# Gate and up of an FFN by seven quarter products, with the order of three engines written out

## The chip, the cores and the metric

One core of a Trainium2 chip runs the whole program in one launch. The metric is the device time of the program in microseconds, from runs on the chip; the profile is one more execution, recorded by the hardware profiler. The core has five engines with queues of their own: TensorE (PE, with its weight loads as PEld), VectorE (DVE), ScalarE (ACT), GpSimd (POOL) and SyncE (SP); here SP and POOL mainly issue transfers.

## The reference

A decoder trunk of two layers, 512 tokens of 1024 features, float32. Layer 0 has a state-space mixer, layer 1 an attention; each is followed by the same gated FFN with 2816 inner features. Only the FFN is touched:

```python
def conv_ffn(h, w_up, conv_w, conv_b, w_down):
    gu = h @ w_up
    g = gu[..., :D_FF]
    u = gu[..., D_FF:]
    g = lax.conv_general_dilated(      # causal, width 3, each feature for itself
        g, conv_w, ..., feature_group_count=D_FF) + conv_b
    return (jax.nn.silu(g) * u) @ w_down
...
x = x + conv_ffn(rms_norm(x, norm_ffn[layer]), ...)
```

After layer 0 a shared key and value are projected from x; after layer 1 a last RMSNorm gives the output.

## The kernel before

Everything is stored feature by token: `x` is 8 tiles of 128 features by 512 tokens. Every matrix product is done to float32 precision by three float32r matmuls for each 128x128 block: an operand is split into a high part (a ScalarE CAST, `split_hi`, L161, or a copy) and a low part (a VectorE subtraction, `split_lo`, L166), and `gemm` (L171) adds high x high, high x low and low x high in a PSUM bank. All these matmuls have line L112 in the profile, all two-input VectorE operations L118 (`tt`) or L115 (`stt`), the CASTs of weights L163.

The 2816 inner features are 22 tiles `f` of 128, handled in three chunks of 8, 7 and 7 (`FF_CHUNKS`). For each tile of a chunk the gate weights `wg` (128 x 1024, 512 KB) are loaded on SP's queue into one of three raw buffers, split, and multiplied with the eight split tiles of x (`bg`, tile fg: 24 matmuls of 512 columns); then the same for up (`wu`, `bu`, tile fu). VectorE multiplies the gate by the RMS factor `rb` of each token (g), ScalarE and VectorE run the filter (acc: one ScalarE operation, two VectorE ones), ScalarE the SiLU (s), VectorE multiplies by rb and s (u), and the product is split again (ah, al) as input of the down product. After a chunk, eight down products (`wd`, tile fd) take the chunk's 8 or 7 tiles as inputs, and each is added to one of the tiles of x. In the last chunk each finished x tile is handed on at once: to the squares for the next norm, and to its own split.

In all this the order of each engine's instructions, and which buffer is reused when, comes from a scheduler that the program runs through when it is built. Two places have an order written out by hand (`tc.manual_schedule`): the sweep of attention, and the end of the kernel, `Final.last` (L1371), where the last two down products are cut into halves of the sequence so that norm and output of the first half run beside the products of the second. Split weights live in rings of three buffers for the high and three for the low parts (pool `wp`): a fourth split waits until TensorE is done with the first.

Of the kernel before, what the change touches and what calls it, by code (L numbers as in the profile page):

```python
# [17 lines left out]
P = 128  # L18
# [1 line left out]
KT = 8  # L20
NH = 16
FT = 22
FF_CHUNKS = ((0, 8), (8, 15), (15, 22))
EPS = 1e-6
AW = 22
TP = {"ta": 10}
# [21 lines left out]
def trunk(ctx: ExitStack, tc: tile.TileContext, A, out):  # L48
# [49 lines left out]
    def wide(name, n, tag):  # L98
        pool, bufs = cur["w"]
        return pool.tile([P, n * S], F32, tag=tag, name=name, bufs=bufs[tag])  # L100

    def N(name, tag, bufs):
# [14 lines left out]
    def tt(o, a, b, op, eng=None):  # L117
        (eng or V).tensor_tensor(out=o, in0=a, in1=b, op=op)  # L118
# [694 lines left out]


    def ffn(layer, prev, st_next):
        with Work(f"ff{layer}", {"g": "la", "s": "lb", "u": "lc"}, a=24, acc=2, y=1, half=6):
            banks_by_tag(b=7, st=1)
            rb, _ = prev.st.finish()
            ffn_body(layer, prev.xs, rb, st_next)

    def ffn_body(layer, xs, rb, st_next):
        cw = const.tile([P, FT, 4], F32, name="cw")
        nc.scalar.dma_start(out=cw, in_=A["conv"][layer])
        for ci, (f0, f1) in enumerate(FF_CHUNKS):
            acts = []
            for f in range(f0, f1):
                wg = load_split(A["w_up"][layer, f, 0], 8, name="wg")
                bg = B("fg")
                gemm(bg, wg, xs)
                wu = load_split(A["w_up"][layer, f, 1], 8, name="wu")  # L830
                bu = B("fu")
                gemm(bu, wu, xs)
                g = T("g", tag="g")
                tt(g, bg, rb, MUL)
                acc = T("acc", tag="acc")
                SC.activation(out=acc, in_=g, func=AF.Identity, scale=cw[:, f, 2:3], bias=cw[:, f, 3:4])  # L836
                stt(acc[:, 1:], g[:, :S - 1], cw[:, f, 1:2], acc[:, 1:], MUL, ADD)
                stt(acc[:, 2:], g[:, :S - 2], cw[:, f, 0:1], acc[:, 2:], MUL, ADD)
                s = T("s", tag="s")
                SC.activation(out=s, in_=acc, func=AF.Silu)  # L840
                u = T("u", tag="u")
                tt(u, bu, rb, MUL)
                tt(u, u, s, MUL)
                ah, al = T("ah", F32R, "a"), T("al", F32R, "a")
                SC.copy(out=ah, in_=u)
                tt(al, u, ah, SUB)
                acts.append((ah, al))
            for n in range(KT):
                w = load_split(A["w_dn"][layer, n][:, f0 * P:f1 * P], f1 - f0, name="wd")
                if f1 == FT and n == KT - 2 and hasattr(st_next, "last"):  # L850
                    st_next.last((w, load_split(A["w_dn"][layer, KT - 1][:, f0 * P:f1 * P], f1 - f0, name="wd")), acts)
                    return
                bd = B("fd")
                gemm(bd, w, acts)
                tt(x[:, n], x[:, n], bd, ADD)
                if ci == len(FF_CHUNKS) - 1:
                    st_next(n)


    def attention(prev, st_next):  # L860
# [495 lines left out]
    class Final:  # L1356
# [7 lines left out]
        def __call__(self, n):  # L1364
            self.st.add(n)
            if n == 0:
                tc.keep_in_program_order(SC.preload_act_table_set("abs_reciprocal_sqrt_and_small"))
                self.y = wide("yo", KT, "y").rearrange("p (k t) -> p k t", k=KT)
            SC.activation(out=self.y[:, n], in_=x[:, n], func=AF.Copy, scale=gcol(NFIN, n))

        def last(self, ws, acts):  # L1371
            n0, H, K = KT - 2, S // 2, len(acts)
            halves = [slice(0, H), slice(H, S)]
            sq6, sq7, v, r, q, rr = (T(t, tag="half") for t in ("sq6", "sq7", "v7", "r7", "q7", "rr7"))
# [40 lines left out]
            with tc.manual_schedule(engines={E.PE, E.DVE, E.Activation}):  # L1415
# [2 lines left out]
                gathered(n0, 0)  # L1418
                product(n0 + 1, 0)
                added(n0 + 1, 0)  # L1420
                mm(total[:, halves[0]], ones, acc[:, halves[0]], True, False)
                product(n0, 1, 0, 5)
                mm(total[:, halves[0]], ones, sq[n0 + 1][:, halves[0]], False, True)
                root(0)
                product(n0, 1, 5, K)
                newton(0)
                added(n0, 1)
                gathered(n0, 1)
                scaled(0, 0, 4)
                send(0, 0, 4, nc.sync)  # L1430
                product(n0 + 1, 1, 0, 4)
                mm(total[:, halves[1]], ones, acc[:, halves[1]], False, False)
                product(n0 + 1, 1, 4, K)
                added(n0 + 1, 1)
                scaled(0, 4, 6)
                send(0, 4, 6, nc.sync)
                mm(total[:, halves[1]], ones, sq[n0 + 1][:, halves[1]], False, True)
# [91 lines left out]
```

## Time and profile before

| | |
|---|---|
| median of 3 runs | 1229.63 us (1229.43 to 1229.68) |
| profiled execution | 1230.19 us |
| its span, first to last instruction | 1228.4 us |
| TensorE busy | 1204.6 us, 98% of the span |
| VectorE busy | 804.0 us, 65% |
| ScalarE busy | 546.0 us, 44% |
| GpSimd busy | 24.0 us, 2% |
| moved by DMA | 118.47 MB, 96 GB/s over the span |
| clock granted to TensorE | 0.998 |

In the profile FFN layer 0 lies at 222 to 584 us, attention at 584 to 853 us, FFN layer 1 from 853 us to the end. A row of the groups gives line, engine, operation, output<-inputs, shape, count, then busy time and mean duration of one, then the idle time before it and what ended that. A row of the chain or of the instructions in order of time gives start and duration in us. A matmul's duration contains its way through the array, so that of neighbours overlaps; the distance between their starts tells what each costs.

### The profile page before, as it was taken

The page shows a single profiled execution, that of the slowest core. Times are in us where ns is not written, and L with a number is a line of the kernel's source. Part 1 is how long each engine was busy: PE and PEld are TensorE (multiplying, and loading weights), DVE is VectorE, ACT ScalarE, POOL GpSimd, SP SyncE. Part 2 cuts the span into 40 slices and gives each one's busy share as a digit, 9 for nine tenths or more (in the row PEclk, how much of TensorE's full clock was granted, in tenths as well). Part 3 has the DMA queues.
Part 4 walks back from the last instruction along what each step waited for, and adds up shares of the span by engine and source line. Part 5 has one row for each costly group of instructions (what it writes and reads, how often), then busy time and mean ns, then how long its engine had stood idle before and what let it go on. Part 6 is the DMA issues. An engine that isn't in the chain of part 4 may idle for free.

```text
span 1228.4 us, 16234 instructions
## 1 busy us (share of the span) xinstructions
PE 1204.6 (98%) x6434; PEld 984.1 (80%) x6434; DVE 804.0 (65%) x1254; ACT 546.0 (44%) x881; POOL 24.0 (2%) x65
## 2 busy tenths in 40 slices
PE   7999999999999999999999999999999999999996
PEld 3467788788888888888889898988888888888885
DVE  7999665655445635657878989878655346536554
ACT  5245453433223323334577878765433233313341
POOL 1011010000000000000000000000000000000000
PEclk9999999999999999999999999999999999999999
DMA  5565342223333233233211211123233332332322
GB/s 195 157 174 146 111 136 89 89 98 103 89 100 103 81 108 103 87 96 104 68 52 54 82 52 51 39 86 103 87 103 93 96 103 85 91 116 86 97 76 69
DMA packets 55037, 118.47 MB, mean 96 GB/s; under 512 B 12881, under 2 KB 28497, under 8 KB 54961
## 3 DMA queue, kind: packets, MB, share of 16 engines
q1 hardware_dynamic: 50304, 105.02, 28.2%
q0 software_dynamic: 3248, 11.54, 3.1%
q8 instruction: 50, 0.82, 0.3%
q10 hardware_dynamic: 1408, 0.88, 0.2%
q14 instruction: 27, 0.21, 0.1%
HBM read 109.03 MB, written 8.39 MB: 96 GB/s over the span
## 4 chain that ended last, share of the span: by engine, by line
PE 88%; DVE 8%; ACT 1%; issue 1%; DMA 1%; DVEq 0%; SPq 0%; ACTq 0%
PE fu L112 19%; PE fd L112 19%; PE fg L112 19%; PE gl L112 6%; PE kqb L112 6%; PE ob L112 5%; PE z L112 5%; PE v L112 4%; PE u L112 2%; DVE k L118 2%; DVE p L118 1%; PE y L112 1%; DMA x<-in_xT 1%; DVE cm L118 1%; ACT xg L282 1%
## 5 line engine op out<-in xcount | busy, mean ns | idle before, releaser
L112 PE MATMUL fd<-ah,wdh 128*128 128x512 f32 (+1 forms) x366 | 140.0, 382 | 0.0
L112 PE MATMUL fd<-al,wdh 128*128 128x512 f32 (+1 forms) x366 | 139.4, 381 | 0.0
L112 PE MATMUL fd<-ah,wdl 128*128 128x512 f32 (+1 forms) x366 | 139.4, 381 | 0.0
L118 DVE TENSOR_TENSOR x<-x,fd 128x512 f32<-128x512 f32 (+1 forms) x50 | 33.3, 665 | 116.6 <-PE fd L112 116.6
L163 ACT CAST wuh<-wur 128x1024 fp32r<-128x1024 f32 x44 | 46.3, 1053 | 134.0 <-PE fg L112 117.8
L163 ACT CAST wdh<-wdr 128x896 fp32r<-128x896 f32 (+1 forms) x48 | 47.2, 983 | 123.8 <-PE fd L112 91.5
L118 DVE TENSOR_TENSOR g<-fg,rb 128x512 f32<-128x512 f32 x44 | 30.4, 691 | 96.3 <-PE fg L112 93.6
L112 PE MATMUL fu<-xh,wuh 128*128 128x512 f32 x220 | 86.0, 391 | 0.0
L112 PE MATMUL fg<-xh,wgl 128*128 128x512 f32 x220 | 85.7, 389 | 0.0
L112 PE MATMUL fu<-xl,wuh 128*128 128x512 f32 x220 | 85.6, 389 | 0.0
L112 PE MATMUL fg<-xh,wgh 128*128 128x512 f32 x220 | 85.6, 389 | 0.0
L112 PE MATMUL fu<-xh,wul 128*128 128x512 f32 x220 | 85.6, 389 | 0.0
L112 PE MATMUL fg<-xl,wgh 128*128 128x512 f32 x220 | 85.6, 389 | 0.0
L118 DVE TENSOR_TENSOR u<-fu,rb 128x512 f32<-128x512 f32 x44 | 30.4, 691 | 80.5 <-PE fu L112 80.5
L112 PE MATMUL fu<-xhl,wuh 128*128 128x512 f32 x264 | 81.9, 391 | 0.0
L112 PE MATMUL fg<-xhl,wgh 128*128 128x512 f32 x264 | 81.6, 389 | 0.0
L112 PEld LDWEIGHTS fd<-ah,wdh 128*128 128x128 f32 x366 | 68.8, 188 | 13.3
L112 PEld LDWEIGHTS fd<-ah,wdl 128*128 128x128 f32 x366 | 68.8, 188 | 13.3
L112 PEld LDWEIGHTS fd<-al,wdh 128*128 128x128 f32 x366 | 68.8, 188 | 13.2
L163 ACT CAST wgh<-wgr 128x1024 fp32r<-128x1024 f32 x44 | 46.3, 1053 | 70.1 <-PE fd L112 32.6
L112 PE MATMUL u<-xg,wi 128*128 128x512 f32 x128 | 64.0, 635 | 7.3 <-ACT xg L282 7.3
L115 DVE SCALAR_TENSOR_TENSOR acc<-g,cw,acc 128x511 f32<-128x511 f32 x88 | 65.7, 747 | 2.5 <-ACT acc L836 0.9
(250 smaller groups left out, 2798.0 us busy)
## 6 DMA issues: line engine op xcount, KB each, us to landing
wgr<-in_w_up SPq DMA_DIRECT2D x44, 512.0 KB, 3.5
wur<-in_w_up SPq DMA_DIRECT2D x44, 512.0 KB, 3.5
wdr<-in_w_dn SPq DMA_DIRECT2D x32, 448.0 KB, 3.3
wdr<-in_w_dn SPq DMA_DIRECT2D x16, 512.0 KB, 3.5
wvr<-in_w_glu POOLq DMA_DIRECT2D x12, 512.0 KB, 3.8
ks<-kx SPq DMA_DIRECT2D x32, 128.0 KB, 2.5
m<-ks SPq DMA_DIRECT2D x8, 512.0 KB, 4.3
awr<-in_w_k SPq DMA_DIRECT2D x8, 512.0 KB, 3.4
```

The costliest lines, as they stand in the source:

```text
L112: PE.matmul(o, lhsT=lhsT, rhs=rhs, start=start, stop=stop, skip_group_check=True)
L115: (eng or V).scalar_tensor_tensor(out=o, in0=a, scalar=s, in1=b, op0=op0, op1=op1)
L118: (eng or V).tensor_tensor(out=o, in0=a, in1=b, op=op)
L163: SC.copy(out=hi, in_=raw)
L282: SC.activation(out=xg.rearrange("p (j c) -> p j c", j=8), in_=by_step(x[:, k]), func=AF.Copy, scale=gcol(NMIX0, k))
```

## The change

Five of the 22 tiles of a layer stay as they were (`Plain`). For the other 17 (`Seven`) gate and up are computed together. With the inner sum cut into two halves of four x tiles, the weights of a tile are four quarters of 128 x 512: A and B (gate), C and D (up). With the tokens cut into two halves of 256, the 2 x 2 block product of quarters and halves of x needs eight products of quarters in the plain way; the change uses a scheme with seven, on sums:

- Weight sums. `Diag` loads A and D side by side by one transfer on SP (`wdg`); their difference is a VectorE subtraction (`differ`), split into dd. `Sum` makes C+A and C+D (`wsa`), and A+B and B+D (`wsb`), by two transfers on POOL's queue: one loads C (or B) twice, and a second, accumulating one (`accum_op=ADD`) adds A and D to it in SBUF. Sums have three buffers of their own (tag sr).
- Sums of x. `form_sums(k)`, for k = 0 to 3, normalizes tiles k and k+4 of x (gain and rb) and forms seven sums and differences of their quarters, 256 columns each; `form_hi` and `form_lo` split them into `fh` and `fl`. It runs beside the plain tiles.
- Products. `first` to `fifth` issue seven products of 4 x 3 matmuls with 256 columns into halves of two banks (f0, f1); some accumulate on the result of an earlier one. VectorE and ScalarE join them to g and u (`sum1`, the ends of `second` and `fourth`, `join`). rb is already in the sums.
- Chunks are now 4, 5, 4, 5 and 4 tiles (`FF_ENDS`), so there are 40 down products with 4 or 5 inputs per layer in place of 24 with 7 or 8. The down products of a chunk are no longer done in one go: four of the first chunk's stand behind the first four tiles, the others stand among the changed tiles of the next chunk (`da` between second and third, `db` at the end), two of the fourth chunk's behind them, and the last chunk's eight end the layer as before.
- The order of TensorE, VectorE and ScalarE is written out from the second plain tile to the end of the changed ones. The loads stay three ahead of the splits (`ahead`).
- In `Final.last` the output and scratch tiles use the buffers of fh and fl, and the order of a few steps is another: the first half's scaling and sending stand behind the products of the second.

```diff
-FF_CHUNKS = ((0, 8), (8, 15), (15, 22))
+FF_ENDS = (4, 9, 13, 18, 22)
...
+        def quarters(f, rows, half, step):
+            o = A["w_up"][layer, f, rows, :, half * Q:half * Q + Q]
+            return bass.AP(o.tensor, o.offset, [[KT * P, P], [step, 2], [1, Q]])
+        diag = P * KT * P + Q
...
+        class Diag(Weight):
...
+            def load(self):
+                self.raw = self.tile()
+                nc.sync.dma_start(out=self.raw.rearrange("p (h c) -> p h c", h=2), in_=quarters(self.f, 0, 0, diag))
+            def differ(self):
+                self.d, dd = T("d", tag="s"), pair("dd")
+                tt(self.d, self.raw[:, 0:Q], self.raw[:, Q:], SUB)
+                self.dw = dd[:, 0:S], dd[:, S:]
...
+        class Sum(Weight):
...
+            def load(self):
+                self.raw = self.tile()
+                t2 = self.raw.rearrange("p (h c) -> p h c", h=2)
+                GP.dma_start(out=t2, in_=quarters(*self.at, 0))
+                GP.dma_start(out=t2, in_=quarters(self.at[0], 0, 0, diag), accum_op=ADD)
+
+        def form_sums(k):
+            q, c = (pair(n, F32).rearrange("p (s c) -> p s c", s=4) for n in ("fq", "fc"))
+            gain = NFFN0 if layer == 0 else NFFN1
+            for i, kk in ((1, k), (0, k + 4)):
+                stt(q[:, i::2], x[:, kk].rearrange("p (s c) -> p s c", s=2), gcol(gain, kk),
+                    rb.rearrange("p (s c) -> p s c", s=2), MUL, MUL)
+            tt(c[:, 0:2], bc(q[:, 1], 1, [P, 2, H]), q[:, 2:4], ADD)
+            tt(c[:, 2], q[:, 3], q[:, 2], SUB)
+            tt(c[:, 3], q[:, 0], q[:, 2], ADD)
+            tt(q[:, 0], q[:, 0], q[:, 1], SUB)
+            form_sums.parts = k, ((c, slice(3, 7)), (q[:, 0:3], slice(0, 3)))
...
+        class Seven(Act):
+            def __init__(self, f, ci):
+                super().__init__(f, ci)
+                self.s1, self.r = Sum(f, 1, 0, "wsa"), Diag(f)
+            def later(self):
+                self.s2 = Sum(self.f, 0, 1, "wsb")
+            def prod(self, o, wt, s, first=False, last=True):
+                gemm(o, wt, [(fh[:, k, s], fl[:, k, s]) for k in range(4)], k1=4,
+                     first=None if first else False, last=None if last else False)
+            def first(self):
+                b0, b1 = B("f0"), B("f1")
+                self.up1, self.gate2, self.m17, self.n6 = b0[:, 0:H], b0[:, H:], b1[:, 0:H], b1[:, H:]
+                self.prod(self.up1, self.s1.part(1), 1, True, False)
+                self.prod(self.gate2, self.r.part(0), 5, False, False)
+                m, tw, self.u = (T(n, tag="u") for n in ("m3", "tw", "u"))
+                self.t, self.wv = tw[:, 0:H], tw[:, H:]
+                SC.copy(out=m[:, 0:H], in_=self.gate2)
+                self.m = m
+            def sum1(self):
+                tt(self.t, self.up1, self.m[:, 0:H], ADD)
+            def second(self):
+                self.prod(self.m17, self.r.dw, 3, True, False)
+                self.prod(self.n6, self.s1.part(0), 4)
+                tt(self.wv, self.m17, self.t, ADD)
+                tt(self.u[:, H:], self.n6, self.wv, SUB)
+            def third(self):
+                self.prod(self.up1, self.r.part(1), 0)
+            def fourth(self):
+                self.prod(self.gate2, self.s2.part(0), 2)
+                self.g = T("g", tag="g")
+                SC.copy(out=self.g[:, H:], in_=self.gate2)
+                tt(self.t, self.t, self.up1, SUB)
+                tt(self.t, self.t, self.gate2, SUB)
+            def fifth(self):
+                self.prod(self.m17, self.s2.part(1), 6)
+            def join(self):
+                tt(self.g[:, 0:H], self.m17, self.t, ADD)
...
+            for t, nxt in zip(sevens, sevens[1:] + [None]):
+                if prev:
+                    prev.mul()
+                if t.da:
+                    t.da.w.hi()
...
+                else:
+                    t.s2.lo()
+                    t.first()
+                    if prev:
+                        prev.split()
+                    t.sum1()
+                if prev:
+                    prev.low()
...
+                t.second()
...
+                if t.da:
+                    t.da.step()
+                    t.da.add()
+                t.third()
+                if t.db:
+                    t.db.w.both()
+                if nxt:
+                    nxt.s1.hi()
+                t.fourth()
+                if nxt:
+                    nxt.s1.lo()
+                t.fifth()
+                if nxt:
+                    nxt.r.hi()
+                    nxt.r.differ()
+                t.join()
+                t.filter0()
+                if t.db:
+                    t.db.step()
+                if nxt:
+                    nxt.r.lo()
+                    nxt.r.differ_hi()
+                    if not nxt.da:
+                        nxt.s2.hi()
+                t.filter()
+                if nxt:
+                    nxt.r.differ_lo()
+                prev = t
```

Three places of the new order, each before and after. L118 and L115 of the kernel before are L122 and L119 of the changed one, and L918 and L919 are the two transfers of `Sum.load`.

First, VectorE in the middle of a chunk of layer 0. Before, one gate-and-up tile after another:

```order
L118 TENSOR_TENSOR g<-fg,rb 128x512
L118 TENSOR_TENSOR wul<-wur,wuh 128x1024
L115 SCALAR_TENSOR_TENSOR acc<-g,cw,acc 128x511
L115 SCALAR_TENSOR_TENSOR acc<-g,cw,acc 128x510
L118 TENSOR_TENSOR u<-fu,rb 128x512
L118 TENSOR_TENSOR u<-u,s 128x512
L118 TENSOR_TENSOR wgl<-wgr,wgh 128x1024
L118 TENSOR_TENSOR al<-u,ah 128x512
```

Now, from the end of one changed tile with one down product into the next (f_2956 and f_2957 are its two banks, wsa the next tile's first sum, wdg its diagonal quarters, d and dd their difference):

```order
L122 TENSOR_TENSOR tw<-tw,f_2956 128x256 x2
L122 TENSOR_TENSOR wsal<-wsar,wsah 128x1024
L122 TENSOR_TENSOR d<-wdgr 128x512
L122 TENSOR_TENSOR g<-f_2957,tw 128x256
L122 TENSOR_TENSOR wdgl<-wdgr,wdgh 128x1024
L119 SCALAR_TENSOR_TENSOR acc<-g,cw,acc 128x511
L119 SCALAR_TENSOR_TENSOR acc<-g,cw,acc 128x510
L122 TENSOR_TENSOR dd<-d,dd 128x512
L122 TENSOR_TENSOR u<-f_2956,s 128x256
L122 TENSOR_TENSOR u<-u,s 128x256
L122 TENSOR_TENSOR wsbl<-wsbr,wsbh 128x1024
```

The splits of the next tile's weights moved in between the joins and the filter of this tile, and the SiLU's product u behind them.

Second, VectorE at the start of layer 0's FFN, from the first tile's g. Before:

```order
L118 TENSOR_TENSOR g<-fg,rb 128x512
L118 TENSOR_TENSOR u<-fu,rb 128x512
L118 TENSOR_TENSOR wgl<-wgr,wgh 128x1024
L115 SCALAR_TENSOR_TENSOR acc<-g,cw,acc 128x511
L115 SCALAR_TENSOR_TENSOR acc<-g,cw,acc 128x510
L118 TENSOR_TENSOR g<-fg,rb 128x512
```

Now (fq and fc are parts of the sums of x):

```order
L122 TENSOR_TENSOR g<-fg,rb 128x512
L122 TENSOR_TENSOR u<-fu,rb 128x512
L119 SCALAR_TENSOR_TENSOR fq<-x,par,rb 128x2x256
L119 SCALAR_TENSOR_TENSOR acc<-g,cw,acc 128x511
L119 SCALAR_TENSOR_TENSOR fq<-x,par,rb 128x2x256
L119 SCALAR_TENSOR_TENSOR acc<-g,cw,acc 128x510
L122 TENSOR_TENSOR fc<-fq 128x512
L122 TENSOR_TENSOR fc<-fq 128x256 x2
L122 TENSOR_TENSOR fq<-fq 128x256
```

The split of the next gate's weights, third before, moved behind the sums of the first pair of x tiles.

Third, POOL's queue from the last weights of the mixer on, with what each waits for (DMASW are the landings of its own transfers). Before:

```order
L143 DMA wvr<-in_w_glu 128x1024 [waits DMASW7_49,DVE_49]
L143 DMA wvr<-in_w_glu 128x1024 [waits DMASW0_49,DVE_49]
L143 DMA wvr<-in_w_glu 128x1024 [waits DMASW1_49,DVE_49]
L1027 MEMSET kl_4755 64x512 [waits DVE_49,PE_49,Pool_49]
L1027 MEMSET kl_4756 64x512
L1027 MEMSET kl_4759 64x512
```

Now:

```order
L147 DMA wvr<-in_w_glu 128x1024 [waits DMASW1_49,DVE_49]
L918 DMA wsar<-in_w_up 128x2x512 [waits PE_49]
L918 DMA wsbr<-in_w_up 128x2x512
L918 DMA wsar<-in_w_up 128x2x512
L919 DMA wsar<-in_w_up 128x2x512 [waits DMASW5_49]
L919 DMA wsbr<-in_w_up 128x2x512 [waits DMASW6_49]
L919 DMA wsar<-in_w_up 128x2x512 [waits DMASW7_49,DMASW2_49]
L918 DMA wsbr<-in_w_up 128x2x512 [waits DMASW3_49,DMASW0_49,DVE_49]
L919 DMA wsbr<-in_w_up 128x2x512 [waits DMASW4_49,DMASW3_49]
L918 DMA wsar<-in_w_up 128x2x512 [waits DMASW1_49,DVE_49,Activation_49]
L919 DMA wsar<-in_w_up 128x2x512 [waits DMASW5_49]
```

Behind the mixer's weights stood only clears for attention; now there are two transfers for each sum, the second waiting for the landing of the first, and a new sum's first waiting for the splits that free its buffer.

More of the change, by code (lines that the diff above doesn't have):

```diff
@@ L822, in ffn_body @@
+    def ffn_body(layer, xs, rb, st_next, fp):
         cw = const.tile([P, FT, 4], F32, name="cw")
         nc.scalar.dma_start(out=cw, in_=A["conv"][layer])
-        for ci, (f0, f1) in enumerate(FF_CHUNKS):
-            acts = []
-            for f in range(f0, f1):
[L827 to L857, printed above, removed]
@@ new lines, in ffn_body, with __init__, step, add @@
+        class Down:
+            def __init__(self, ci, n):
+                self.ci, self.n, (self.f0, self.f1) = ci, n, chunks[ci]
+                self.w = Weight("wd", self.f1 - self.f0, A["w_dn"][layer, n][:, self.f0 * P:self.f1 * P])
+            def step(self, k0=0, k1=9):
+                k1 = min(k1, self.f1 - self.f0)
+                if k0 == 0:
+                    self.b = B("fd")
+                last = k1 == self.f1 - self.f0
+                gemm(self.b, [t[:, k0 * P:] for t in self.w.w], acts[self.ci][k0:], k1=k1 - k0,
+                     first=None if k0 == 0 else False, last=None if last else False)
+            def add(self):
+                tt(x[:, self.n], x[:, self.n], self.b, ADD)
@@ new lines, in ffn_body @@
+        lead = 4
+        plains = [Plain(f, 0) for f in range(*chunks[0])]
+        leads = [Down(0, n) for n in range(lead)]
+        plains.append(Plain(chunks[1][0], 1))
+        sevens, spare = [], []
+        for ci, (f0, f1) in enumerate(chunks[1:], 1):
+            n = lead if ci == 1 else 0
+            f0 += ci == 1
+            last = ci == len(chunks) - 1
+            places = [(f, 1) for f in range(f0, f1)] + [(f, 0) for f in range(f0 + 2 * last, f1, 1 if f1 - f0 < 5 else 2)]
+            places = places[:KT - n]
+            for f in range(f0, f1):
+                t = Seven(f, ci)
+                sevens.append(t)
+                t.da = t.db = None
+                for i, name in enumerate(("da", "db")):
+                    if (f, i) in places:
+                        setattr(t, name, Down(ci - 1, n))
+                        n += 1
+                t.later()
+            spare = [Down(ci - 1, k) for k in range(n, KT)]
@@ L860, in attention @@
+        ci, (f0, f1) = len(chunks) - 1, chunks[-1]
+        for n in range(KT):
+            w = load_split(A["w_dn"][layer, n][:, f0 * P:f1 * P], f1 - f0, name="wd")
+            if n == KT - 2 and hasattr(st_next, "last"):
+                st_next.last((w, load_split(A["w_dn"][layer, KT - 1][:, f0 * P:f1 * P], f1 - f0, name="wd")), acts[ci])
+                return
+            bd = B("fd")
+            gemm(bd, w, acts[ci])
+            tt(x[:, n], x[:, n], bd, ADD)
+            st_next(n)
     def attention(prev, st_next):
@@ L1373, in last @@
             halves = [slice(0, H), slice(H, S)]
-            sq6, sq7, v, r, q, rr = (T(t, tag="half") for t in ("sq6", "sq7", "v7", "r7", "q7", "rr7"))
+            half = forms_tile("half")
+            sq6, sq7, v, r, q, rr = (half[:, i * S:i * S + S] for i in range(6))
             sq = {n0: sq6, n0 + 1: sq7}
```

222 lines of the change are left out of this document (210 added, 12 removed).

## The prediction

> **What bounds the kernel now.** I read the page's busy times and its chain of waits first, then the chain in order of time around layer 0's FFN, then single rows on the engines that the change loads.
>
> ```profile
> span 1228.4 us, 16234 instructions
> PE 1204.6 (98%) x6434; PEld 984.1 (80%) x6434; DVE 804.0 (65%) x1254; ACT 546.0 (44%) x881; POOL 24.0 (2%) x65
> PE 88%; DVE 8%; ACT 1%; issue 1%; DMA 1%; DVEq 0%; SPq 0%; ACTq 0%
> ...
> 246.96 5.44 PE fg L112 x24
> 252.40 5.44 PE fu L112 x24
> ...
> 546.16 38.08 PE fd L112 x168
> 584.24 3.17 PE kqb L112 x14
> ...
> 595.43 0.86 PE rbp L112 x2
> ...
> 603.20 1.72 PE z L112 x11
> ```
>
> TensorE is 88% of the chain, and in the FFN nothing else is on it: gate and up stand back to back, 24 matmuls in 5.44 us, so one of 512 columns costs 226.7 ns. (The 389 ns that the groups print for it is longer than this distance; I use distances.) What takes work off TensorE there is won in full, as long as the other engines keep up.
>
> ```profile
> 355.80:431.90 76.10, 76.10 (x337) 63.01 (x336) 43.75 (x54) 27.77 (x35) 0.00 (x0) 1.00 0.30 93
> 546.20:584.20 38.00, 38.00 (x169) 31.46 (x168) 27.75 (x35) 17.56 (x25) 0.00 (x0) 1.00 0.34 105
> ```
>
> Busy time by stretch (TensorE, weight loads, VectorE, ScalarE, GpSimd, clock, DMA share): through seven gate-and-up tiles VectorE is busy 43.75 of 76.10 us; through the last down products of layer 0, 27.75 of 38.00.
>
> **Term 1, the products.** A changed tile has 7 x 12 = 84 matmuls of 256 columns in place of 48 of 512. The trace has such matmuls, with new weights before each, in the end of layer 1 and in attention:
>
> ```profile
> 1205.09 0.28 PE L112 MATMUL fd<-ah,wdh 128*128 128x256 f32 x1
> 1207.25 0.28 PE L112 MATMUL fd<-ah,wdh 128*128 128x256 f32 x1
> 651.87 5.81 PE v L112 x48
> L112 PEld LDWEIGHTS fd<-ah,wdh 128*128 128x128 f32 x366 | 68.8, 188 | 13.3
> ```
>
> Eighteen steps lie between the first two rows: 120 ns each; the v stretch gives 121. So half the columns cost 53% of the time. A tile: 48 x 226.7 = 10.88 us before, 84 x 120 = 10.08 after, 0.80 less; 34 tiles (17 in each layer): **-27.2 us**. At 121 it is -24.4. The down products keep their matmuls; the last four, cut into halves of the sequence, are shorter (four inputs instead of seven): 36 half matmuls become 18 whole ones, **-0.2**.
>
> The Trainium skill (TensorE: Matmul & The Clock Gate, "Wait — 56ns, not 53.3ns?") has start-to-start at columns over 2.4 GHz plus about 2.5 ns, an estimate of 215.8 and 109.2 ns for the two sizes. By it a tile would save 1.19 us and the whole 40, a time of 1195; both of this kernel's distances are longer than the page's, so I give that 1 in 100.
>
> **Term 2, the steady changed tile.** Per tile VectorE now splits two weight sums, the diagonal quarters and their difference, and joins the products. The chain that must close within a tile is the first place shown in the change's order: the splits for the next tile's first products stand behind the joins of this one. Prices, from VectorE's and ScalarE's rows in order of time and ScalarE's groups:
>
> ```profile
> 654.40 0.41 DVE L115 SCALAR_TENSOR_TENSOR t<-z,t 128x256 f32<-128x256 f32 x1
> 654.74 0.41 DVE L1083 CAST lh<-t 128x512 fp32r<-128x512 f32 x1
> ...
> 657.74 0.68 DVE L118 TENSOR_TENSOR vt<-v,sr 128x512 f32<-128x512 f32 x1
> 658.34 1.21 DVE L118 TENSOR_TENSOR awl<-awr,awh 128x1024 fp32r<-128x1024 f32 x1
> 659.48 0.75 DVE L118 TENSOR_TENSOR vv<-vt,vv 128x256 fp32r<-128x256 f32 x2
> ...
> 363.24 1.53 DVE L115 SCALAR_TENSOR_TENSOR acc<-g,cw,acc 128x511 f32<-128x511 f32 x2
> 366.68 0.69 DVE L118 TENSOR_TENSOR u<-fu,rb 128x512 f32<-128x512 f32 x1 [1.91 <-PE fu L112]
> 367.47 0.69 DVE L118 TENSOR_TENSOR u<-u,s 128x512 f32<-128x512 f32 x1
> L1072 ACT ACTIVATE t<-t 128x256 f32<-128x256 f32 x32 | 13.5, 421 | 0.2
> L836 ACT ACTIVATE acc<-g,cw 128x512 f32<-128x512 f32 x44 | 35.7, 811 | 0.8 <-DVE g L118 0.8
> L163 ACT CAST wgh<-wgr 128x1024 fp32r<-128x1024 f32 x44 | 46.3, 1053 | 70.1 <-PE fd L112 32.6 <-PE fu L112 28.1 <-PE gl L112 8.9
> ```
>
> 256 elements hold VectorE for 0.34 us, 512 for 0.60, 1024 for 1.14; a dependent follower waits 0.19 more; the filter pair takes 1.45. One tile with one four-wide down product: three 1024-splits 3.42, five of 512 (d, dd, al, x, wdl) 3.0, eight of 256 (two mul, sum1, wv, u, two of t, join) 2.72, filter 1.45, dependents 0.6: 11.2 us, against 10.08 + 12 x 0.2267 = 12.8 on TensorE. So it fits, if the waits do. The tightest: the sixth product ends 8.6 + 0.2 us into the tile, ScalarE's copy 0.42, then t, t, wsal, d, join, wdgl, filter, dd = 0.34 + 0.53 + 1.14 + 0.60 + 0.34 + 1.14 + 1.45 + 0.69: 15.4. TensorE wants the low part of dd in the third matmul of the next tile's third product, at 12.8 + 2.9 + 0.2 = 15.9. I take **0**, with 0.4 us to spare. Sixteen tiles have one down product, twelve of them four wide; the eighteen with two (15.5 and 16.9 us) have more room. If each of the sixteen missed by 0.5: +8.
>
> ScalarE sums to some 7.5 us per tile (three CASTs of 1.05, the rest shorter), covered by TensorE's 12.8; its in-order queue holds the SiLU behind wsbh, which waits for the previous down product to free a weight slot, but mul comes later anyway (VectorE is in dd).
>
> **Term 3, the plain tiles.** Five tiles stay plain, and VectorE forms the sums of x beside them (the second place shown): the next gate's split now stands behind them. From the first g there to the first changed tile's third product VectorE has 12 ops of 1024 (13.7), 4 of 768 (3.5), 39 of 512 (23.4), 12 of 256 (4.1), five filter pairs (7.3), some 16 dependents (3.0): 55 us. TensorE's room: plain tiles two to five 43.5, four lead products 10.9, two products and a bit 3.1: 57.5 from the second gate, and VectorE starts just ahead of it:
>
> ```profile
> 235.55 0.69 DVE L118 TENSOR_TENSOR g<-fg,rb 128x512 f32<-128x512 f32 x1 [1.90 <-ACT rb L228]
> 235.90 0.40 PE L112 MATMUL fg<-xh,wgh 128*128 128x512 f32 x1
> 239.75 1.28 ACT L840 ACT_TABLE_LOAD   x1 [2.06 <-DVE acc L115]
> 862.81 0.69 DVE L118 TENSOR_TENSOR g<-fg,rb 128x512 f32<-128x512 f32 x1 [0.76 <-ACT rb L228]
> 866.10 0.39 PE L112 MATMUL fg<-xh,wgh 128*128 128x512 f32 x1
> ```
>
> Its waits for ScalarE's high halves (the table load, 1.9 us where the third gate's CAST stands behind two CASTs of sums and a SiLU, 1.2 at the first lead) bring my walk to 60.4: **+3** in layer 0 (between 0, if they overlap better, and +6). In layer 1 the g is 3.3 us ahead of the gate instead of 0.35: **0**.
>
> **Term 4, the seams.** Layer 0's last downs now last 8 x 2.72 = 21.8 us for the work that filled 27.75, less 3.9 us of narrower splits: VectorE runs late into attention. There k, q and v products, all still available, stand ahead of the first z; before, they and rbp filled 603.20 - 584.24 = 19 us. **+1** (0 to +3). At the end of the kernel the last product is added 2 us late, behind the first half's Newton steps, and its sums wait behind the scaling; the shorter products give most back.
>
> ```profile
> 1217.90 0.42 DVE L118 TENSOR_TENSOR x<-x,fd 128x256 f32<-128x256 f32 x1 [0.72 <-PE fd L112]
> 1220.07 0.42 DVE L124 TENSOR_SCALAR v<-sum 128x256 f32<-128x256 f32 x1 [0.35 <-ACT r L1394]
> ```
>
> 2.2 us lie between these two; I count 3.0 after: **+0.5** (-0.5 to +1.5).
>
> **Term 5, the accumulating transfers.** The trace has none. POOL's queue, idle in the FFN before, now issues a plain transfer, waits for it, and issues the accumulating one (the third place). Behind the waiting one stands the next sum's first transfer, which can go once the first has landed.
>
> ```profile
> wvr<-in_w_glu POOLq DMA_DIRECT2D x12, 512.0 KB, 3.8
> ...
> c<-in_c SPq DMA_DIRECT2D x1, 768.0 KB, 12.1
> 12.00:14.00 2.00, 2.00 (x3) 0.64 (x3) 1.97 (x20) 2.00 (x4) 0.00 (x0) 1.00 1.04 428
> ```
>
> A pair takes 7.6 us if accumulating costs nothing more, 15.9 with the slowest landing of the trace. Three buffers serve two sums a tile, and one is held some 4.3 us (from the high split to the end of the low): a tile lasts at least (pair + 4.3) / 1.5, which reaches 12.8 at a pair of 14.9. I take 10, nearer the plain row of the same bytes: **0**; at 15.9, (20.2 / 1.5 - 12.8) x 12 = +8. In bytes a tile loads 2.9 MB, at most 3.9 with the sums read back: 305 GB/s in 12.8 us, under the 428 of the start's window. The Trainium skill (Collectives: The Full Stack, "The bandwidth ceiling: the fold count and why AG ≠ RS ≠ AR") says that an add in the DMA path halves the rate because it reads two sources; by it a pair would be about 9.5 us as an estimate, and the sum unchanged; no run here shows it.
>
> **Sum.** -27.2 - 0.2 + 3 + 0 + 1 + 0.5 = -22.9. The profiled execution took 1230.19, of which 1.8 us lie outside the span: 1207.3; it stands 0.56 over the median of the runs: 1206.7. **I predict 1207.**
>
> **Rivals.** *VectorE becomes the bound* at the plain tiles and in the tiles with one down product: the 0.4 us and the 3 us are small beside some 50 hand-counted waits. At 0.8 us over in twelve tiles and +6 at the start: 1207 + 10 + 3 = 1220. For it: 11.2 of 12.8 us busy in a strict order. Against: the two-down tiles let it catch up. *Accumulation is slow* (the other side): at the POOL pair of wsa and wsb a pair of 18 us holds a tile at 14.9: 12 x 2.1 + 4 x 1.4 (five wide, 13.5 us) = +30, 1237; it decides from about 17.3 us, where all 22.9 are gone. Against: no landing of the trace, even in its densest burst, is long enough. *Half-width matmuls don't hold their distance* in so dense a row: at the 188 ns of a weight load, 84 x 188 = 15.8 us, +167; the v stretch, with a load before each, speaks against. *The gain goes in many small waits*: 1230, no change.
>
> **Chances.** Forecast 0.62 (own range 1201 to 1215), VectorE bound 0.18, slow accumulation 0.12, the page's shorter steps 0.01, half-width 0.02, no change 0.05. Bounds: the low ends of the terms give 1229.6 - 27.4 - 0.5 = 1201.7; the high ends of terms 1 to 4 give 1229.6 - 24.6 + 8 + 6 + 3 + 1.5 = 1223.5, and all of term 5 too 1231.5. Range 1200 to 1226. This kernel's times tell 0.2%, 2.5 us, from no change. Faster 0.81, same 0.05, slower 0.14.
>
> **What would show it.** Changed tiles with one down product 12.8 us apart in the chain, at 120 ns a matmul: term 1 right. TensorE waiting for dd or wdgl at the tile's third product: term 2 wrong; for fl or wdgl at the first changed tile, term 3. ScalarE waiting for DMA wsar or wsbr: accumulation. A pair's landing times give the missing price. The forecast is wrong if the changed stages show TensorE idle for over 10 us together.

## The result, and the profile after

The changed kernel takes 1316.42 us (median of four runs, 1312.09 to 1324.70) where the kernel before takes 1229.66: a ratio of 1.071, 95% interval 1.065 to 1.076. It is 87 us slower; 1207 had been predicted, with 14% on slower. The profiled execution took 1312.09.

The head of its page, its chain by engine, one group of ScalarE and the landing times of the weight sums:

```profile
span 1310.3 us, 19584 instructions
PE 1213.0 (93%) x7640; PEld 1032.3 (79%) x7640; DVE 971.5 (74%) x1654; ACT 631.4 (48%) x1065; POOL 155.2 (12%) x201
...
PE 39%; issue 27%; DVE 18%; POOL 6%; DMA 5%; ACT 4%; POOLq 0%; DVEq 0%; SPq 0%; ACTq 0%
...
L167 ACT CAST wsah<-wsar 128x1024 fp32r<-128x1024 f32 x34 | 35.7, 1050 | 140.1 <-DMA wsar<-in_w_up 131.5
...
wsar<-in_w_up POOLq DMA_DIRECT2D x68, 512.0 KB, 7.5
wsbr<-in_w_up POOLq DMA_DIRECT2D x68, 512.0 KB, 6.7
```

TensorE was 88% of the chain and is 39% now. "Issue" (27%), POOL and DMA have come in, and ScalarE's split of wsa stood still for 131.5 us in all, waiting for the transfer. Where the 82 us of the span lie, busy time by stage (stretch, TensorE, weight loads, VectorE, ScalarE, GpSimd, clock, DMA share, GB/s), before:

```profile
222.00:584.00 362.00, 361.51 (x1596) 298.53 (x1595) 202.90 (x259) 126.14 (x154) 0.00 (x0) 1.00 0.31 96
584.00:853.00 269.00, 268.88 (x1563) 238.11 (x1562) 227.49 (x387) 198.09 (x378) 2.14 (x4) 1.00 0.21 63
853.00:1228.40 375.40, 364.20 (x1646) 302.30 (x1645) 201.75 (x267) 125.92 (x155) 0.00 (x0) 0.99 0.30 93
```

and after, cut where layer 0's FFN and attention end there:

```profile
222.00:628.80 406.80, 368.83 (x2210) 325.69 (x2209) 282.54 (x454) 167.18 (x245) 65.62 (x68) 0.98 0.59 150
628.80:902.00 273.20, 269.75 (x1564) 238.66 (x1564) 231.96 (x393) 200.00 (x381) 7.84 (x10) 1.00 0.26 76
902.00:1310.30 408.30, 364.16 (x2238) 322.56 (x2237) 285.06 (x466) 168.41 (x247) 59.88 (x62) 0.98 0.56 143
```

Layer 0's FFN is 45 us longer and layer 1's 33, attention 4. TensorE stands idle for 38 and 44 us in the two FFNs (under 1 and 11 before), and DMA is at 56 to 59% of its engines' time: over a stage nothing is full. What happens instead is seen on POOL in order of time (start, duration, transfer, idle before it and what ended that), in the middle of layer 0. L918 is a sum's plain transfer, L919 its accumulating one:

```profile
456.72 1.19 POOL L919 DMA_DIRECT2D wsar<-in_w_up  x1 [6.95 <-DMA wsar<-in_w_up]
458.07 0.74 POOL L918 DMA_DIRECT2D wsbr<-in_w_up  x1 [0.17 <-issue]
465.58 1.18 POOL L919 DMA_DIRECT2D wsbr<-in_w_up  x1 [6.76 <-DMA wsbr<-in_w_up]
466.31 1.20 POOL L918 DMA_DIRECT2D wsar<-in_w_up  x1
475.30 1.19 POOL L919 DMA_DIRECT2D wsar<-in_w_up  x1 [7.79 <-DVE wsbl L122]
476.03 1.21 POOL L918 DMA_DIRECT2D wsbr<-in_w_up  x1
```

One sum every 9 to 10 us: POOL issues the accumulation, at once the next sum's plain transfer, and then stands until that has landed. (The row at 475.30 names VectorE, but its plain transfer landed at 475.02; 64 of the 68 accumulations start 0.3 us behind the landing of their own plain transfer.) From the fourth accumulation of a layer to the last, the distance is 9.49 us in layer 0 (294.36 to 578.93, 30 sums) and 9.22 in layer 1. The plain transfer lands 8.1 us after its issue (median of the 68), though the same 512 KB took 3.8 on POOL's queue before. Busy time in half-microseconds from 442 on shows why (the last two columns are DMA share, which goes by the packets' time and can pass 1, and GB/s):

```profile
442.00:442.50 0.50, 0.50 (x7) 0.50 (x6) 0.00 (x0) 0.00 (x0) 0.00 (x0) 1.00 1.13 209
443.00:443.50 0.50, 0.50 (x6) 0.46 (x5) 0.00 (x0) 0.00 (x0) 0.00 (x0) 1.00 1.11 205
...
444.50:445.00 0.50, 0.50 (x4) 0.42 (x3) 0.00 (x0) 0.43 (x1) 0.00 (x0) 1.00 0.98 365
445.00:445.50 0.50, 0.50 (x4) 0.38 (x4) 0.00 (x0) 0.50 (x1) 0.00 (x0) 1.00 0.99 381
```

The accumulation that was issued at 438.61 moves first, at 205 GB/s with the DMA engines full. The plain transfer issued 0.7 us after it comes behind it, together with a load of wdg that SyncE issued at 440.41: the last two rows, 365 and 381 GB/s, are the two queues' sum. The chain of waits says how TensorE is reached (start, duration, what):

```profile
391.77 0.76 POOL wsar L918
392.53 8.86 issue
401.40 7.47 DMA wsar<-in_w_up
...
409.90 0.37 ACT g L1034
410.30 0.43 DVE tw L122
...
411.18 0.06 DVE wsal L122
```

The 8.86 us of "issue" are POOL's wait for the landing of the plain transfer, so the chain is: the plain transfer, the accumulation, then ScalarE, which has the split of the next wsa at the head of its in-order queue and the copy of this tile's gate quarter behind it; VectorE's t waits for that copy, the low part of wsa for t, and TensorE for the low part.

### The profile page after: what moved, and what is told of

Read it like the earlier page. It is cut to its first block, busy times and chain, and to the rows that moved or that the text cites. A ratio compares the mean times of both kernels' runs of the same rounds, so it can differ in the third digit from the quotient of the medians.

```text
span 1310.3 us, 19584 instructions
## 1 busy us (share of the span) xinstructions
PE 1213.0 (93%) x7640; PEld 1032.3 (79%) x7640; DVE 971.5 (74%) x1654; ACT 631.4 (48%) x1065; POOL 155.2 (12%) x201
## 4 chain that ended last, share of the span: by engine, by line
PE 39%; issue 27%; DVE 18%; POOL 6%; DMA 5%; ACT 4%; POOLq 0%; DVEq 0%; SPq 0%; ACTq 0%
PE gl L116 6%; PE ob L116 5%; PE fd L116 5%; PE f L116 5%; PE kqb L116 4%; PE z L116 4%; PE v L116 3%; PE fu L116 2%; DMA wsar<-in_w_up 2%; PE u L116 2%; DMA wsbr<-in_w_up 2%; POOL wsbr L919 2%; POOL wsar L919 2%; PE fg L116 2%; DVE k L122 2%
## 5 line engine op out<-in xcount | busy, mean ns | idle before, releaser
L122 DVE TENSOR_TENSOR tw<-tw,f 128x256 f32<-128x256 f32 x68 | 28.6, 421 | 137.4 <-ACT g L1034 136.2
L167 ACT CAST wsah<-wsar 128x1024 fp32r<-128x1024 f32 x34 | 35.7, 1050 | 140.1 <-DMA wsar<-in_w_up 131.5
L116 PE MATMUL f<-fh,wdgh 128*128 128x256 f32 x272 | 79.8, 293 | 24.3 <-DVE tw L122 24.3
L116 PE MATMUL f<-fh,wsal 128*128 128x256 f32 x272 | 79.5, 292 | 19.8 <-DVE wsal L122 19.8
L116 PE MATMUL f<-fh,wdgl 128*128 128x256 f32 x272 | 81.5, 300 | 8.4 <-DVE wdgl L122 8.3
L116 PE MATMUL f<-fh,wsah 128*128 128x256 f32 x272 | 77.4, 285 | 3.0 <-ACT wsah L167 3.0
L116 PE MATMUL f<-fl,wsah 128*128 128x256 f32 x272 | 77.5, 285 | 2.3 <-DVE fl L122 2.3
L116 PE MATMUL f<-fh,wsbh 128*128 128x256 f32 x272 | 78.9, 290 | 0.0
L116 PE MATMUL f<-fl,wsbh 128*128 128x256 f32 x272 | 78.5, 289 | 0.0
L116 PE MATMUL f<-fh,wsbl 128*128 128x256 f32 x272 | 78.5, 289 | 0.0
L116 PE MATMUL f<-fl,wdgh 128*128 128x256 f32 x272 | 78.5, 289 | 0.0
L116 PEld LDWEIGHTS f<-fh,wdgh 128*128 128x128 f32 x272 | 53.5, 197 | 27.4 <-DVE tw L122 26.7
L122 DVE TENSOR_TENSOR x<-x,fd 128x512 f32<-128x512 f32 (+1 forms) x82 | 54.3, 669 | 25.4 <-PE fd L116 25.2
L918 POOL DMA_DIRECT2D wsar<-in_w_up x34 | 37.6, 1107 | 289.4 <-PE ob L116 248.1
```

What stands on the lines that cost most here:

```text
L116: PE.matmul(o, lhsT=lhsT, rhs=rhs, start=start, stop=stop, skip_group_check=True)
L167: SC.copy(out=hi, in_=raw)
L918: GP.dma_start(out=t2, in_=quarters(*self.at, 0))
```

## The experiments

A run given with one number is one execution. The kernel with the plain transfers on SyncE, run six times more, lay between 1218.44 and 1224.88 us, so a few us between two single runs say little.

**Four kernels that tell the causes apart.** First, the adding transfer is left out:

```diff
                 GP.dma_start(out=t2, in_=quarters(*self.at, 0))
-                GP.dma_start(out=t2, in_=quarters(self.at[0], 0, 0, diag), accum_op=ADD)
```

> Leaves out the second, adding transfer of each of the 68 weight sums, so the sums are wrong and the rest of the work is unchanged. Theory Q (each sum passes POOL's queue alone: accumulation 5.8 us, then the next plain transfer behind it, 9.2 us a sum, 18.4 us a tile) and theory B (three buffers are too few): the waits of ScalarE for wsar and wsbr go, and the time falls from 1312 to 1215-1225: the predicted 1207 plus what the changed kernel lost beside the plain tiles (first changed tile 9 us late in layer 0 and 6 in layer 1 where 3 and 0 were forecast) and at the seam. Theory V (VectorE's order is the bound, one-down tiles at 13.6 us or more): 1230 or above, with TensorE waiting for dd and wdgl.

It took 1222.2 us (the kernel before 1229.3 beside it). All of the loss and more hangs on the sums' transfers. Theory V falls.

Second, a fourth buffer for the sums (`BUFS` is 4 for them and 3 for the rest), and to make room one buffer in place of two for the filter's accumulator:

```diff
-                return pool.tile([P, 8 * P], F32, tag=self.tag, name=self.name + "r", bufs=3)[:, :self.cols * P]
+                return pool.tile([P, 8 * P], F32, tag=self.tag, name=self.name + "r", bufs=BUFS[self.tag])[:, :self.cols * P]
...
-            while st[0] < min(len(q), st[1] + 3):
+            while st[0] < min(len(q), st[1] + BUFS[tag]):
...
-                Work(f"ff{layer}", {"g": "la", "s": "lb", "u": "lc"}, a=8, acc=2, fo=2):
+                Work(f"ff{layer}", {"g": "la", "s": "lb", "u": "lc"}, a=8, acc=1, fo=2):
```

> Four buffers for the weight sums in place of three (and one for the filter's accumulator in place of two, to make room); POOL's order is kept. Theory B, which the prediction's formula stands on (a tile lasts at least (pair + 4.3) / buffers per tile): with a pair of some 15 us and four buffers (15 + 4.3) / 2 = 9.7 us, the bound goes, 1215-1230. Theory Q: no buffer was waited for, 1305-1318, no change.

1288.24: neither. POOL's rows show the same distance in the steady tiles (accumulations at 460.45, 469.98, 479.29, 488.35 and 498.01, 9.4 us apart), so the rate did not move and theory B is wrong as a bound; but one sum more lies ready when the changed tiles begin, and the kernel runs dry later: of layer 0's tiles the first three distances stay at 12.8 to 13.1 us, where in the change only the first did. Q had missed that a store shortens the loss.

Third, the order on POOL's queue (flush issues the accumulation of the sum before):

```diff
                 GP.dma_start(out=t2, in_=quarters(*self.at, 0))
-                GP.dma_start(out=t2, in_=quarters(self.at[0], 0, 0, diag), accum_op=ADD)
+                flush()
+                pend.append((t2, self.at[0]))
```

> POOL issues the plain transfer of the next sum ahead of the accumulating one of this sum; transfers and buffers are the same. Theory Q: while one sum's plain transfer lands, the accumulation before it is under way, so a sum costs one landing of some 6 us in place of 9.2, a tile 13 to 14.5: 1225-1255. Theory B: the buffers still bind, and the accumulation now starts later, 1300 or above. Theory R (the accumulating transfers' rate on the DMA engines, 205 GB/s, is the bound): no change, 1300-1318.

1326.02, as B had it and 8 us over R's range, but it tells nothing: the order on the engine shows each accumulation right behind its own plain transfer again. The scheduler sets POOL's order (only TensorE, VectorE and ScalarE are written out), and it had moved them back. The fourth has another queue for the plain transfers:

```diff
-                GP.dma_start(out=t2, in_=quarters(*self.at, 0))
+                nc.sync.dma_start(out=t2, in_=quarters(*self.at, 0))
```

> The plain transfers of the sums go on SyncE's queue, the accumulating ones stay on POOL's. Theory Q: a plain transfer no longer waits for an accumulation, POOL issues one 5.8 us accumulation a sum, 11.6 us a tile at most: 1218-1235. Theory B: 1300 or above, as the buffers are the same. Theory R: 1300-1318.

1221.88, as Q had it: with the same bytes, buffers and accumulations, all of the loss is gone. R and B both fall. The plain transfers land after 5.1 us there (median) in place of 8.1. The Trainium skill (DMA: Bandwidth & Descriptors, Queues, rings and completion order) has each DMA engine take turns between queues packet by packet; the half-microsecond from 445.50 agrees, with 33 packets of POOL's queue and 31 of SyncE's. The accumulations now stand 7.48 us apart in either layer, which is what TensorE asks for: one sum every 7.4 us, half of the mean tile of 14.8. The changed tiles themselves are seen in ScalarE's SiLU, one a tile, at three tiles with one down product:

```profile
310.85 0.63 ACT L960 ACTIVATE s<-acc 128x512 f32<-128x512 f32 x1 [0.30 <-DVE acc L119]
323.67 0.63 ACT L960 ACTIVATE s<-acc 128x512 f32<-128x512 f32 x1 [0.29 <-DVE acc L119]
336.49 0.63 ACT L960 ACTIVATE s<-acc 128x512 f32<-128x512 f32 x1 [0.29 <-DVE acc L119]
```

12.82 us each. And TensorE's waits in this kernel from layer 0's first changed tile to the end of its FFN are four in all (waiting line, releaser, us in total, times, longest):

```profile
PE f L116 <- DVE fl L122: 1.1, 1, 1.1
PE fd L116 <- ACT wdh L167: 0.9, 1, 0.9
PE f L116 <- DVE wdgl L122: 0.4, 1, 0.4
PE f L116 <- DVE dd L122: 0.3, 1, 0.3
```

**Order, or the adding itself?** The third kernel again with POOL's order held as written:

```diff
-                GP.dma_start(out=t2, in_=quarters(*self.at, 0))
+                tc.keep_in_program_order(GP.dma_start(out=t2, in_=quarters(*self.at, 0)))
```

(and the same for the accumulation).

> As the run with the next plain transfer first, but with POOL's order held to the order written: there the compiler's scheduler had put each accumulation right behind its own plain transfer again, so the order on the queue had not moved. Theory Q (one sum at a time through POOL's queue, 9.2 us each): two sums are under way, and a tile falls from 18 us to 13-14.5: 1225-1255. Theory S (one DMA queue carries all of POOL's transfers one after another, so order does not matter): 1290 or above.

1239.01: Q; theory S falls. Four fifths of the 94 us against the fourth kernel were POOL's order alone. What is left against the fourth kernel, 17 us, is in the main 6.8 us of waits for t in layer 0 and 6.3 in layer 1; the accumulation now stands behind the next plain transfer, which waits for its buffer.

Then the order of the change, with the second transfer plain:

```diff
-                GP.dma_start(out=t2, in_=quarters(self.at[0], 0, 0, diag), accum_op=ADD)
+                GP.dma_start(out=t2, in_=quarters(self.at[0], 0, 0, diag))
```

> The second transfer of each sum is plain as well: it overwrites in place of adding, so the sums are wrong; order, waits, bytes and buffers are as in the change. If the wait between the two transfers is what costs (theory Q), a sum still takes 1.9 us of issues and a landing of 4.5 to 6, 13 to 16 us a tile against 12.8 wanted: 1235-1270. If the adding itself is what costs (theory A, 205 against 350 GB/s): 1220-1226, as without the second transfer.

1219.44: below what Q expected, and 0.6 us under theory A's range. POOL in this kernel:

```profile
455.17 0.72 POOL L919 DMA_DIRECT2D wsar<-in_w_up  x1 [4.79 <-DMA wsar<-in_w_up]
455.89 0.70 POOL L918 DMA_DIRECT2D wsbr<-in_w_up  x1
461.23 0.72 POOL L919 DMA_DIRECT2D wsbr<-in_w_up  x1 [4.64 <-DMA wsbr<-in_w_up]
461.94 0.70 POOL L918 DMA_DIRECT2D wsar<-in_w_up  x1
467.94 0.72 POOL L919 DMA_DIRECT2D wsar<-in_w_up  x1 [5.30 <-DMA wsar<-in_w_up]
```

The wait is still there, but in these rows a sum takes 6.1 to 6.7 us in place of 9.2 to 9.5, under the 7.4 that are asked. So with the run before it takes both: an accumulation that holds the queue some 2.8 us longer than a plain transfer (0.5 in its issue, 2.3 until the plain transfer behind it has landed, 8.1 us after its issue in place of 5.7, medians), and an order that puts the next sum's first transfer behind it and the next accumulation behind that.

**Adding on GpSimd instead.** The diagonal quarters lie in SBUF anyway; the other quarter is loaded once and added there:

```diff
-                t2 = self.raw.rearrange("p (h c) -> p h c", h=2)
-                GP.dma_start(out=t2, in_=quarters(*self.at, 0))
-                GP.dma_start(out=t2, in_=quarters(self.at[0], 0, 0, diag), accum_op=ADD)
+                f, rows, half = self.at
+                nc.sync.dma_start(out=self.raw[:, 0:Q], in_=A["w_up"][layer, f, rows, :, half * Q:half * Q + Q])
...
+            def add(self, d):
+                for h in (1, 0):
+                    tt(self.raw[:, h * Q:h * Q + Q], d[:, h * Q:h * Q + Q], self.raw[:, 0:Q], ADD, GP)
...
+                    nxt.s1.add(nxt.r.raw)
+                    nxt.s2.add(nxt.r.raw)
                     nxt.s1.hi()
```

> No accumulating transfer: the off-diagonal quarter is loaded once by SyncE (256 KB in place of 1 MB a sum), and GpSimd adds it to the diagonal quarters that lie in SBUF already, two adds of 512 a sum. If GpSimd takes under 3 us an add (four a tile, 12.8 us) and leaves VectorE's operations at their 0.34, 0.60 and 1.14 us: 1218-1226. If it slows VectorE beside it, whose 11.2 of 12.8 us leave no room: 1240 or above, with TensorE waiting for dd and wdgl.

1292.81. GpSimd takes 1.68 us an add, as was asked of it, but VectorE pays: two groups of VectorE by shape between 320 and 560 in this kernel,

```profile
L122 DVE TENSOR_TENSOR dd<-d,dd 128x512 fp32r<-128x512 f32 x15 | 17.7, 1183 | 0.0
...
L122 DVE TENSOR_TENSOR x<-x,fd 128x512 f32<-128x512 f32 x23 | 15.7, 682 | 3.6 <-PE fd L116 3.6
```

and in the kernel with the plain transfers on SyncE, between 320 and 550:

```profile
L122 DVE TENSOR_TENSOR x<-x,fd 128x512 f32<-128x512 f32 x24 | 16.4, 683 | 9.1 <-PE fd L116 9.1
...
L122 DVE TENSOR_TENSOR dd<-d,dd 128x512 fp32r<-128x512 f32 x15 | 10.3, 685 | 0.0
```

The split with both inputs in SBUF goes from 685 to 1183 ns; the add that has one input in PSUM stays at 682. TensorE waits 18.7 us for dd in layer 0 and 20.5 in layer 1, and 6 in each for fl. The Trainium skill (SBUF — State Buffer, "Who interferes with whom") says that a GpSimd operation that reads SBUF and a VectorE operation with two SBUF inputs lock one pair of ports against each other; the rows agree. From SiLU to SiLU the 16.92 us (two five-wide down products) stay, while layer 0's first three 12.82 become 14.4, 16.8 and 15.0 and its 15.56 become 18.3: the loss lies where there was little room, and the 0.4 us to spare in the one-down tiles are gone.

Forming the sums of x on GpSimd (on top of the plain transfers on SyncE), the other expectation on term 3:

```diff
-            tt(c[:, 2], q[:, 3], q[:, 2], SUB)
+            tt(c[:, 2], q[:, 3], q[:, 2], SUB, GP)
```

(four such lines)

> Plain transfers on SyncE's queue as in the run that reached 1221.9, and the four sums of each of the four steps that form the seven inputs are added by GpSimd in place of VectorE. This prices term 3: VectorE loses some 1.8 us of work in each of four steps, and TensorE's waits at the first changed tile (3 us in layer 0, 3 to 4 in layer 1, with 1.5 at the leads) shrink: 1214-1220. If GpSimd's adds take over 1.5 us each the chain to the high parts gets longer instead: 1224-1232.

1227.36: GpSimd's adds took 1.70 us (512) and 0.85 to 0.91 (256), over the point named, and the chain to the high parts got longer. TensorE's wait for fl is gone, as the theory had it, but it now waits earlier, at the leads and the last plain gate.

**The kernel that stays, timed, and what it still loses.**

> The kernel with the plain transfers on SyncE's queue once more, for its interval against the kernel before: 1220-1224 by its one time of 1221.9 (before 1229.3), a ratio of 0.993 to 0.995. By the prediction's sum, with accumulation at 0 as forecast, 1207; the 13 to 17 us between would be the small waits seen in its trace: at the leads and the first changed tile (4.5 us in layer 0, 4 in layer 1), 1.5 ahead of the last downs of each layer, 4 in attention, 1 to 3 at the end.

1220.50 us (median of six, 1218.44 to 1224.88) against 1230.40: a ratio of 0.992, interval 0.990 to 0.994. That is 0.8% faster than before, and 13.5 us above the forecast. Then two edits at the waits that are left. Of the four adds of the leads (the down products ahead of the first changed tile), one goes behind the first changed tile's second() and two behind its mul, where the second tile's turn begins; and the split of the first spare down product's weights goes ahead of the last filter:

```diff
-            for d in leads:
-                d.add()
+            leads[0].add()
...
+                if t is sevens[1]:
+                    leads[2].add()
+                    leads[3].add()
...
+                if t is sevens[0]:
+                    leads[1].add()
...
+                if not nxt:
+                    spare[0].w.both()
                 t.filter()
...
```

> On top of the plain transfers on SyncE's queue: three of the four adds of the lead down products move from ahead of the first changed tile's splits to behind them, and the split of the first spare down product's weight goes ahead of the last filter. If VectorE's order there is what TensorE waits for (term 3), the first changed tile's waits shrink from 2.9 us in layer 0 and 3.9 in layer 1 to under 1.5 each and the 1.5 us ahead of the last downs go in both layers: 5 to 7 us, 1214-1218. If those waits are covered elsewhere or come back later (the rival of many small waits), the time stays within 2 us of the other kernel: 1219-1224.

1225.37, ratio 0.995 (0.994 to 0.997): slower than without the edits. The waits for fl, wdgl and, ahead of the last downs, wdh are gone, but a new one has come in each layer, on TensorE in order of time:

```profile
309.55 0.55 PE L116 MATMUL f<-fh,wsah 128*128 128x256 f32 x1 [4.04 <-DVE x L122]
```

The two late adds hold the PSUM bank that the second changed tile's first product takes. After this wait TensorE also runs at half its pace (last section): the clock granted is 0.50 from 308.1 to 314.9, and the distance of 12.82 us to the next SiLU becomes 19.45. With two adds left in place, the other two behind the first tile's second(), and the spare split as in the run before:

```diff
-            for d in leads:
+            for d in leads[:2]:
                 d.add()
...
+                if t is sevens[0]:
+                    for d in leads[2:]:
+                        d.add()
```

> As the run before, but two of the four adds stay ahead of the first changed tile and the other two stand behind its third product's splits: there, two adds behind the second tile's u had kept a PSUM bank, and TensorE waited 4.2 us for it in each layer. If that bank was the whole loss, the 4.2 us go in both layers and the gain at the first changed tile and ahead of the last downs stays: 1215-1218. If the two adds push the first tile's own splits (dd, with 0.4 us to spare), TensorE waits there instead: 1218-1221, no gain over the kernel with the plain transfers on SyncE alone.

1215.32 (1213.62 to 1219.58), a ratio to the kernel before of 0.989, interval 0.987 to 0.991: the lowest of all here, though the interval overlaps the end of that without the edits (0.990 to 0.994). TensorE's waits from its first changed tile to 575 in layer 0:

```profile
PE f L116 <- DVE wdgl L122: 0.4, 1, 0.4
PE f L116 <- DVE dd L122: 0.4, 1, 0.4
```

## Why the prediction was wrong

**Term 5 failed**, and it was the whole of the sign. The pair was priced at 10 us with 15.9 as its end; it measures 13.9 (8.1 for the plain landing, 5.8 for the accumulating one): inside the bounds. The formula was wrong: "a tile lasts at least (pair + 4.3) / 1.5", with its threshold at 14.9, lets one and a half pairs be under way at a time because there are three buffers. By it 13.9 gives a tile of 12.1, no loss. But the text ahead of it names what forbids that: behind the waiting accumulation stands the next sum's first transfer. So a second bound had to be worked out, that of the queue: a sum lasts the issue of an accumulation and the landing of the plain transfer behind it, 1.2 + 8.1 = 9.3 us here, against the 7.4 that a mean tile allows. Only its size was not to be had from the trace before (with a plain landing of 3.8 it is 5.0, and harmless); its form was, and it would have put the point from which the term decides at a landing of 6.2, between the rows of 3.8 and 12.1, in place of a pair of 14.9. The rival of slow accumulation had the right place and side, and 1237 for its size, by the same formula; but its condition, a pair of 17.3 us or more, was not met.

From the first changed tile's SiLU to the last one's, layer 0 takes 288.2 us (310.27 to 598.45) against 237.0 with the plain transfers on SyncE, layer 1 278.3 against 237.0: 92.4 us, where the two spans differ by 90.3. TensorE also ran at half its pace after some of the waits (below). No step had that, but it is not shown to add to the loss: POOL goes from one sum to the next on the landings alone, so in the main it falls into time that TensorE would have waited.

The Trainium skill (Collectives: The Full Stack, "The bandwidth ceiling: the fold count and why AG ≠ RS ≠ AR"), which says it of ReduceScatter, was quoted for an add in the DMA path that halves the rate. Here it nearly does: 205 GB/s, where in the run without the adding transfer POOL's queue alone, with the engines full, moves 370 (median of half-microseconds). The pair of 9.5 us that was worked out from it is too short: the accumulation lands after 5.8 us, near the 5.7 that are in it, but the plain transfer waits for its turn.

**Terms 1 and 2 held**, once the sums were on time: 120 ns from one 256-column matmul to the next in the changed tiles, and tiles with one down product 12.82 us apart against 12.8, 0 over. The rivals that VectorE becomes the bound and that half-width matmuls don't hold their distance fall with the same rows; VectorE's 0.4 us to spare was real, as the kernel that took it away (GpSimd's adds) showed.

**Terms 3 and 4 were too small.** In the kernel with the plain transfers on SyncE: at the leads and the first changed tile TensorE loses 4.5 us in layer 0 and 3.9 in layer 1 (3 and 0 forecast; 1.4 of layer 1's is the half pace, 15 matmuls of 93 ns each); attention takes 273.4 in place of 269.0 (+1 forecast); from the last down product to the end 13.8 in place of 10.8 (+0.5 forecast), and VectorE is busy there without a gap from 1206.9 to 1215.7; that the scaling of the first half no longer fits beside the shorter products is read from this and was not tried apart. Not in the sum at all: TensorE waits for the first weight of each layer's last downs, whose split stands behind the last filter's SiLU on ScalarE, 1.5 us a layer by the distances of its matmuls. With these the sum is -27.4 + 4.5 + 3.9 + 4.4 + 3.0 + 3.0 = -8.6: 1230.2 - 8.6 = 1221.6, and 1221.9 was measured. So the rival of many small waits was partly right: with the loss of term 5 gone, they take over half of the 22.9 us. The last run confirms the parts in the tiles and ahead of the last downs in part (5.2 us between the two medians, of 11.4); attention and the end were not tried apart.

Two figures of the prediction are off without bearing on this: with the shorter steps its sum is 1194, not 1195; and the slowest landing of the trace before is 12.6 us (a load of wi at 5.6 us), not 12.1, a pair of 16.4.

## What to carry to other kernels

Where a transfer must wait for another on the queue that issued it, work out two bounds: what the buffers allow, and what the queue allows when the next item stands behind the wait; the larger one decides. Put the dependent transfer and the one that feeds it on different queues before adding buffers, and look at the order that the scheduler really gave that queue. A step that is moved off a critical place can take a PSUM bank with it: follow what the late instruction frees.

## What was not expected of the hardware

After a wait, TensorE ran at half its pace for some 3.6 us. From the changed kernel, the first of a product after 5 us of waiting, and its like 3.7 us later:

```profile
1171.81 0.58 PE L116 MATMUL f<-fh,wdgh 128*128 128x256 f32 x1 [5.09 <-DVE tw L122]
1172.19 0.41 PE L116 MATMUL f<-fl,wdgh 128*128 128x256 f32 x1
1172.40 0.41 PE L116 MATMUL f<-fh,wdgl 128*128 128x256 f32 x1
...
1175.79 0.28 PE L116 MATMUL f<-fl,wsbh 128*128 128x256 f32 x1
1175.91 0.28 PE L116 MATMUL f<-fh,wsbl 128*128 128x256 f32 x1
```

213 ns from start to start, then 120; the clock granted to TensorE is 0.50 from 1168.66 to 1175.49 and 1.00 behind it. 83 matmuls of the changed tiles stand at the longer distance, 7.7 us more than at 120; in the kernel with the plain transfers on SyncE 15 do. The Trainium skill (TensorE: Matmul & The Clock Gate, Part 1) gives columns over 1.2 GHz for an array that has idled through a window of 3.4 us, an estimate of 213.3 ns at 256 columns, and as long to recover; the distance agrees. But the 15 matmuls in layer 1 of the kernel on SyncE fell to it after waits of 1.1 and 0.4 us, shorter than such a window.

The records of the granted clock tell more. Among the changed tiles it is halved for 3.41 us at a time, seven times in the changed kernel (two of them in a row). In the 3.41 us ahead of each, TensorE was busy for 0.26 to 1.68 us, and ahead of the one in the kernel on SyncE (920.00 to 923.40) for 1.86. So several short waits within 3.4 us were enough. No exact limit is shown: a like stretch of the changed kernel with 1.62 us (from 1131.10) was not followed by the half clock.

An accumulating transfer of 512 KB into SBUF held POOL 1.18 us in its issue where a plain one held it 0.72, moved at 205 GB/s where plain ones moved at 370 (median, POOL's queue alone with the engines full), and landed 5.6 us after its issue at best, a plain one on the same queue 3.6.
